# TensorE's order in the attention written out by hand, and other units without adaLN rows, in a hybrid decoder layer on one core

## The chip, the core and the metric

The kernel runs on one core of a Trainium2 chip. A core has several engines that run side by side, each with an instruction stream of its own that it works through in order: TensorE (PE in the profile; PEld is its loading of weights) multiplies matrices and writes into the small memory PSUM, VectorE (DVE) and ScalarE (ACT) do the elementwise work, GpSimd (POOL) does next to nothing here, and SyncE (SP) issues transfers. Streams wait for each other by semaphores. The metric is the device time of one execution in microseconds (us); lower is better.

## What is computed

One decoder layer on a sequence of 256 tokens with a model width of 2048, everything in float32. The reference, cut to what matters here:

```python
mod = jnp.dot(silu(c), w_ada[l]) + b_ada[l]                 # adaLN: 6 x 2048 values
shift1, scale1, gate1, shift2, scale2, gate2 = jnp.split(mod, 6, axis=-1)
h = _modulate(_rms_norm(x, norm1_g[l]), shift1, scale1)
proj = jnp.einsum("bsd,de->bse", h, w_in[l])
lru_x, lru_gate, q, k, v, g_a, g_b = jnp.split(proj, split_idx, axis=-1)
xc = _causal_depthwise_conv(lru_x, conv_w[l], conv_b[l])
rec = _rg_lru(xc, ...)                                      # two gate products, a scan over time
y_a = (rec * gelu(lru_gate)) @ w_lru_out[l]
att = _swa_sink_attention(q, k, v, attn_sinks[l], rel_bias) # 32 query heads, 4 kv heads, window 128
y_b = att @ w_attn_out[l]
merged = sigmoid(g_a) * y_a + sigmoid(g_b) * y_b
x = x + gate1 * (merged @ w_out[l])
h2 = _modulate(_rms_norm(x, norm2_g[l]), shift2, scale2)
x = x + gate2 * (square(relu(h2 @ w_ff1[l])) @ w_ff2[l])
return _rms_norm(x, final_g)
```

The attention adds a bias that depends on the distance, masks what lies outside the window, and its softmax has one more term, a sink value per head.

## The kernel before

**Products.** Activations lie with channels across the 128 partitions and the 256 tokens along the free dimension. For accuracy each float32 operand is split into a rounded part (`wh`, `hl[:, 0]`) and the rest (`wl`, `hl[:, 1]`), and a product is made of three matmuls. `gemm` (lines 196 to 207) does one tile of 128 output channels with three matmuls of 256 columns for each of its tiles of input channels; `gemm_wide` (line 220) does the same with one matmul of 512 columns and one of 256 (lines 229, 230, 232).

**Weights and units.** After a prologue the rest is a list of `units`. A unit takes 1 MB of weights. Its weights are loaded into one of 4 `raw` buffers (line 173, SyncE's queue), and then split in two halves of 1024 columns: ScalarE rounds (`w_round`, line 178, tile `wh`), VectorE takes the rest (`w_rest`, line 183, tile `wl`). `wh` and `wl` have 4 buffers each, so two units' worth. The main loop at the end of the function first loads and splits the weights of unit n + 2 and then runs unit n, so in the order of the program the split stands ahead of the unit's own work.

The prologue has already multiplied the first 8 of the 16 input tiles for the first 60 of 84 output tiles of the input projection. What is left of these goes two output tiles at a time: `gemm_pair` (line 240) calls `gemm` twice, with 24 matmuls each, and the first of the two uses the first half of the weights, the second the second half. The units are numbered so:

| units | what |
|---|---|
| 0, 1 | keys, values |
| 2 to 9 | queries: unit 2 + g gives the queries of group g (4 heads) |
| 10 to 17, 18 to 25 | the two halves of the recurrent branch (`lru_x`, `lru_gate`) |
| 26 to 29, 30 to 37 | first branch gate (pairs, then single wide tiles) |
| 38 to 53 | second branch gate |
| 54 to 69 (`n_ya` = 54) | first output projection, of the recurrent branch |
| 70 on | the attention's output projection, the joint one, the MLP |

**Attention.** For each of 8 groups of 4 heads, `att_scores` (line 651) loads the bias tile `bt` (one buffer, on ScalarE's queue), makes the scores on TensorE (16 instructions, line 669) into four PSUM banks, and the softmax: VectorE adds bias and finds the extreme (line 674), ScalarE takes the exponential (line 677), sums and the reciprocal follow (lines 680 to 683), and VectorE scales by it (line 687, eight instructions). `att_values` (line 691) turns the four heads' probabilities with 12 transposes on TensorE (line 702), which ScalarE copies out of PSUM (line 704), and multiplies them with the values (line 709, 16 instructions): for each pair of heads six transposes, two copies, eight products, one copy of the result (line 711).

**What sets the order.** The function only traces the instructions. A planner then makes each engine's stream: an instruction may be issued when its inputs and buffers are there by the planner's own estimate of times, and of those that may, the one traced earliest goes first. So an instruction can stand in the stream some way off its place in the program. `pin` (`tc.keep_in_program_order`) binds an instruction behind the one traced before it on its engine. In the input projection nothing on TensorE is pinned in the version before.

Elementwise work and the attention are put on a list `side` with a cost (`later`); after each unit the main loop traces from its front as long as there is `credit`, 2.3 per unit, at most 6. A query unit puts `att_values` of the group before (0.3) and `att_scores` of its own (2.5) on it; so in the program the scores of group g stand right after unit 2 + g. The recurrent branch (`lru_conv`, `lru_gates`, `lru_decay`, `lru_scan`, `lru_gelu`) is on the same list.

**Rows.** The 96 rows of the adaLN product are done one by one on VectorE: a row's weights (1 MB) come into one of the same four `raw` buffers (line 109), and one instruction multiplies and sums (`ada_unit`, line 283). The main loop adds a credit for rows with each unit (0.2 for the first 8 units, 0.6 for the next 10, then 0.1 and from unit 28 on 0.5) and issues as many as it covers: their loads ahead of the weights of unit n + 2, their sums after the unit. In quiet units it issues none and the credit stays. Before, the 8 units ahead of `n_ya` are quiet.

**Buffers.** The pool `kp` has 48 tiles (activations, results of the projections), `tp` 9 temporaries, `pa` four PSUM banks for the attention and other small products, `pg` four for the projections. At `n_ya` the recurrent branch's result is split into 16 tiles (`split`, lines 164 to 168) that take the places of the normed input `h`.

Of the kernel before, what the change touches and what calls it, by code (L numbers as in the profile page):

```python
# [12 lines left out]
AF = mybir.ActivationFunctionType  # L13
# [4 lines left out]
P = 128  # L18
# [9 lines left out]
W_IN_ORDER = (list(range(48, 50)) + list(range(50, 52)) + list(range(32, 48)) + list(range(0, 16))  # L28
              + list(range(16, 32)) + list(range(52, 68)) + list(range(68, 84)))
RAW_BUFS, WH_BUFS, WCH = 4, 4, 1024  # L30
LAG, CC, CG, CV, CS = 2, 1, .6, .3, 2.5
SSD = 4
EARLY, WARM = 6, 36

LAG, CC, CG, CV, CS = 2, 1.0, 0.6, 0.3, 2.5

ADA_LAST, QUIET_OUT, QUIET_FF1 = 0.3, 2, 3
LOOK, CREDIT, Z_FROM, QUIET_YA = 2, 2.3, 12, 8
ADA_RATES = 8 * [0.2] + 10 * [0.6] + 10 * [0.1] + 28 * [0.5]

ZN_FROM = 9
# [14 lines left out]
def _done(f):  # L56
    return max([k1 for k0, k1, n in PASSES if f < n], default=0)
# [9 lines left out]
def hybrid_layer(ctx: ExitStack, tc: tile.TileContext, x, xt, wada, w_p, w_r, w_f, vec, lruw, relb,  # L67
                 onehot, maskc, ident, out):
    nc = tc.nc
    te, ve, se = nc.tensor, nc.vector, nc.scalar  # L70
# [19 lines left out]
    def tmp(shape=(P, 2, T), dt=F32):  # L90
        return tp.tile(list(shape), dt, tag="t2", name=nm("t"))

    def bank(shape):
        return pa.tile(list(shape), F32, tag="pa", name=nm("pa"))


    pin = tc.keep_in_program_order
    vc = cp.tile([P, NV], F32, name="vc")
    idt = cp.tile([P, P], F32, name="idt")
# [5 lines left out]
    same = lambda i: i  # L105
# [87 lines left out]
    def w_load(src, n):  # L193
        return w_split(*w_dma(src, n))

    def gemm(parts, o, acts, ps=None):
        if ps is None:
            ps = pg.tile([P, T], F32, tag="pg", name=nm("pg"))
        n = len(acts)
        for k, hl in enumerate(acts):  # L200
            e = (o + k) * P
            wh, wl = parts[e // WCH]
            w = slice(e % WCH, e % WCH + P)
            te.matmul(ps, lhsT=wh[:, w], rhs=hl[:, 0], start=k == 0, stop=False)  # L204
            te.matmul(ps, lhsT=wh[:, w], rhs=hl[:, 1], start=False, stop=False)  # L205
            te.matmul(ps, lhsT=wl[:, w], rhs=hl[:, 0], start=False, stop=k == n - 1)  # L206
        return ps

    def gemm_late(parts, o, acts, pss, late):
# [27 lines left out]
        ve.tensor_tensor(out=t, in0=ps[:, 0], in1=t, op=ALU.add)  # L237
        return t

    def gemm_pair(parts, o, acts):  # L240

        ps = pg.tile([P, 2, T], F32, tag="pg", name=nm("pg"))
        for i in range(2):
            gemm(parts, o + i * len(acts), acts, ps[:, i])
        return ps

    full = [0]
# [46 lines left out]
    for q in range(4):  # L294
        pc = line_quarter(q)
        o = scr[:, q * 512:(q + 1) * 512]
# [39 lines left out]
    h = [None] * KT  # L336
# [114 lines left out]
    res, both = {}, {}  # L451
# [87 lines left out]
    for i in range(FRONT, len(p_units)):  # L539
        k0, k1, u, nf = p_units[i]  # L540
        split_w[i + 1] = split_unit(i + 1)
        w = split_w.pop(i)
# [5 lines left out]
        for j in range(nf if u or not k0 else 0):  # L548
            f = u + j
            if f % 2 == 0:  # L550
                open_ps[0] = pg.tile([P, 2, T], F32, tag="pg", name=nm("pg"))
            ps = open_ps[0][:, f % 2]
# [23 lines left out]
    units, side = [], []  # L576
# [8 lines left out]
    def later(cost, fn, *a):  # L585
        side.append((cost, fn, a))

    def in_unit(f, fin, nf=1):

        kd = _done(f)  # L590
        if kd:
            n = (KT - kd) * nf * P
            src = w_r[w_off[0]:w_off[0] + n * P].rearrange("(p n) -> p n", p=P)
            w_off[0] += n * P

            def run(w):
                if f == 0:
                    ps = pg.tile([P, 2, T], F32, tag="pg", name=nm("pg"))
                    gemm_late(w, 0, h[kd:], [(ps[:, 0], True, False), (ps[:, 1], False, True)], 2)
                    fin(f, ps, both[f])  # L600
                elif nf == 2:
                    fin(f, gemm_pair(w, 0, h[kd:]), both[f])
                else:
                    fin(f, gemm(w, 0, h[kd:]), res[f])
            add_unit(run, src, n)
        else:
            add_unit(lambda w: fin(f, gemm_wide(w, h), None))
# [9 lines left out]
    kd = [cp.tile([P, T], F32, name=f"kd{i}") for i in range(4)]  # L617
    vtok = cp.tile([P, 2, T], F32, name="vtok")
# [30 lines left out]
    ast = {}  # L649

    def att_scores(g):

        kv = g // 2
        bt = sp.tile([P, 4, T], F32, tag="bias", name=nm("bt"), bufs=1)
        se.dma_start(out=bt, in_=bass.AP(tensor=ud.tensor, offset=ud.offset + 4 * g * 384,
                                         ap=[[1, P], [384, 4], [1, T]]))
        st = sp.tile([P, 3, 8], F32, tag="ast", name=nm("as"), bufs=2)
        ng, dn, es = st[:, 0], st[:, 1], st[:, 2]
        ss = []
        sink = nsink[:, 8 * g:8 * g + 8]  # L660
        for t in range(2):
            q = res[F_Q + 2 * g + t]
            pss = [bank([P, 384]) for _ in range(2)]

            for qs, ks, sl in ((slice(0, 128), slice(128, 256), slice(0, 128)),
                               (slice(128, 256), slice(0, 256), slice(128, 384))):
                for i in range(2):
                    hd = slice(64 * i, 64 * i + 64)
                    te.matmul(pss[i][:, sl], lhsT=q[hd, qs], rhs=kd[kv][hd, ks], start=True, stop=True)
            for i in range(2):  # L670
                s = tmp([P, 384])
                for b, sl in HALVES:
                    c = 2 * (2 * t + i) + b
                    ve.tensor_tensor_reduce(out=s[:, sl], in0=pss[i][:, sl], in1=bt[:, 2 * t + i, 0:128 * (b + 1)],
                                            scale=1.0, scalar=sink[:, c:c + 1], op0=ALU.add, op1=ALU.min,
                                            accum_out=ng[:, c:c + 1])
                    table("exp", se.activation(s[:, sl], s[:, sl], AF.Exp, scale=-1.0, bias=ng[:, c:c + 1],
                                               accum_out=dn[:, c:c + 1]))
                ss.append(s)
        ve.tensor_tensor(out=es, in0=ng, in1=sink, op=ALU.subtract)  # L680
        table("exp", se.activation(es, es, AF.Exp))
        ve.tensor_tensor(out=dn, in0=dn, in1=es, op=ALU.add)
        ve.reciprocal(out=dn, in_=dn)
        for i in range(4):
            for b, sl in HALVES:
                c = 2 * i + b
                ve.tensor_scalar(out=ss[i][:, sl], in0=ss[i][:, sl], scalar1=dn[:, c:c + 1], scalar2=None, op0=ALU.mult)
        ast[g] = ss

    def att_values(g):  # L690

        kv = g // 2
        ss = ast.pop(g)
        vs = slice(64 * kv, 64 * kv + 64)
        for t in range(2):
            po = bank([P, T])
            pvs = []
            for i in (2 * t, 2 * t + 1):
                pt = bank([P, 384])

                for n, j in enumerate((0, 2, 1)):
                    te.transpose(pt[:, n * P:(n + 1) * P], ss[i][:, j * P:(j + 1) * P], idt)
                pv = tmp([P, 384])
                se.activation(pv, pt, AF.Copy)
                pvs.append(pv)

            for kb, cols, pc in ((1, slice(0, 256), slice(0, 256)), (0, slice(128, 256), slice(256, 384))):
                for i in range(2):
                    te.matmul(po[64 * i:64 * i + 64, cols], lhsT=vtok[:, kb, vs], rhs=pvs[i][:, pc],  # L709
                              start=kb == 1, stop=kb == 0)  # L710
            se.activation(res[F_Q + 2 * g + t], po, AF.Copy)

    def q_fin(f, ps, part):
        ve.scalar_tensor_tensor(out=part, in0=ps, scalar=-0.125, in1=part, op0=ALU.mult, op1=ALU.add)
        if f > 0:
            later(CV, att_values, f // 2 - 1)
        later(CS, att_scores, f // 2)
        if f == 14:
            later(CV, att_values, 7)


    lw, ri, ys, cv = {}, {}, {}, {}
# [401 lines left out]
    n_ya = len(units)  # L1124
    n_z = n_ya + 32 + Z_FROM
    n_ff1 = n_ya + 48
# [20 lines left out]
    for n, (run, src, size) in enumerate(units):  # L1147
        left = n_z - n
        if n < n_ya:
            ada_credit += size / 2048 * ADA_RATES[n]  # L1150
        else:
            ada_credit += max(0, 5 * KT - ada_next[0]) / left if left > 0 else ADA_LAST
        rows = 0
        if not (n_ya - QUIET_YA <= n < n_ya or n_ff1 - QUIET_OUT <= n < n_ff1 or n_ff1 + 16 - QUIET_FF1 <= n < n_ff1 + 16):
            while ada_credit > rows and ada_next[0] + rows < 6 * KT:
                rows += 1
            ada_credit -= rows
        for _ in range(rows):
            ada_dma()
        for j in range(n, min(n + LOOK + 1, len(units))):  # L1160
            if j not in ready:
                ready[j] = units[j][1]()
        if n == n_ya:
            flush()
        run(ready[n])
        ready[n] = None
        credit = min(credit + CREDIT * size / 2048, 6.0)
        while credit > 0 and side:
            cost, fn, a = side.pop(0)
            fn(*a)  # L1170
            credit -= cost
        while rows > 0 and ada_raw:
            ada_unit()
            rows -= 1
# [91 lines left out]
```

## Time and profile before

| | us |
|---|---|
| median of 3 runs | 1568.23 |
| lowest and highest run | 1567.98, 1568.62 |
| the profiled execution | 1566.39 |
| its span in the profile | 1564.6 |
| VectorE's busy share, ScalarE's | 82%, 59% |
| adaLN rows on VectorE (line 283) | 225.2 for 96, 2.35 each |
| splits of weights, ScalarE and VectorE (lines 178, 183) | 560.6 and 645.0 for 542 each |

How to read it: the profile comes from one execution, and the span is the time from its first to its last instruction; the device time lies a little above. A group of instructions is named by line, engine, operation, and the tiles that it writes and reads (out<-in), with its count. "Idle before" is the time in which the engine rested just before, and the name behind the arrow is what ended the rest. TensorE's matmuls overlap: one that is shown for 0.28 us may start every 0.12 us, so for TensorE the distance between starts tells more than busy time. A row of the windows view has the stretch, its length, then busy time and number of instructions for PE, PEld, DVE, ACT and POOL, TensorE's granted clock, the busy share of the DMA engines, and GB/s. A row of the timeline has start, length, engine, line, operation, tiles; instructions of one kind in a row are merged (x8). A row of the chain of waits has start, length and what it was.

### The profile page before, as it was taken

Reading aid. Unit: us, or ns where it says so; the run is one execution under the profiler, and the core shown is the slowest. Engines: PE = TensorE matmul, PEld = TensorE weight load, DVE = VectorE, ACT = ScalarE, POOL = GpSimd, SP = SyncE. Lnnn points to the kernel's source line nnn. Section 1 sums busy time; section 2 is a strip of 40 time slices with the busy share of each in tenths; the row PEclk is TensorE's granted clock in tenths of the full one; section 3 lists DMA queues with packets and bytes.
Section 4 is the critical chain, followed back from the end, with each engine's and each line's share of the span. In section 5 each row is a group of like instructions: output and inputs, shape, how many; then the busy total and the mean of one; then the engine's idle time right before and its main releaser. Section 6 shows DMA issues by size and latency. Waiting matters only on the chain.

```text
span 1564.6 us, 25672 instructions
## 1 busy us (share of the span) xinstructions
PE 1544.1 (99%) x10137; PEld 1397.7 (89%) x10137; DVE 1285.7 (82%) x2030; ACT 927.5 (59%) x1531; POOL 0.2 (0%) x4
## 2 busy tenths in 40 slices
PE   8999999999999999999999999999999999999998
PEld 7999998899988888888889988888888888888987
DVE  5898987898899689899898877888866888678785
ACT  5753457676786565444466763357644765357664
POOL 0000000000000000000000000000000000000000
PEclk9999999999999999999999999999999999999999
DMA  9998974566668669878987666866554566545551
GB/s 372 362 386 305 367 289 149 192 238 218 227 232 295 227 252 344 320 297 297 336 303 270 245 242 241 309 217 201 202 202 175 175 202 211 188 167 201 189 213 57
DMA packets 84744, 387.93 MB, mean 248 GB/s; under 512 B 7344, under 2 KB 36368, under 8 KB 44432
## 3 DMA queue, kind: packets, MB, share of 16 engines
q1 hardware_dynamic: 79632, 381.51, 66.8%
q10 hardware_dynamic: 4992, 4.79, 0.9%
q8 instruction: 79, 1.29, 0.3%
q14 instruction: 41, 0.34, 0.1%
HBM read 384.13 MB, written 2.15 MB: 247 GB/s over the span
## 4 chain that ended last, share of the span: by engine, by line
PE 90%; DVE 4%; DMA 2%; ACT 2%; issue 1%; ACTq 0%; SPq 0%; DVEq 0%
PE pg L230 40%; PE pg L229 19%; PE pg L206 6%; PE pg L204 5%; PE pg L205 5%; DMA ra<-in_wada_dram 2%; PE pg L232 1%; PE pa L937 1%; PE pa L939 1%; PE pa L938 1%; DVE ra L283 1%; PE pa L709 1%; PE pg L986 1%; PE pg L985 1%; PE pg L984 1%
## 5 line engine op out<-in xcount | busy, mean ns | idle before, releaser
L230 PE MATMUL pg<-k,wh 128*128 128x512 f32 x2832 | 981.4, 394 | 1.1 <-DVE k L167 1.1
L178 ACT ACTIVATE wh<-rw 128x1024 fp32r<-128x1024 f32 (+1 forms) x542 | 560.6, 1041 | 471.4 <-PE pg L230 320.3
L183 DVE TENSOR_TENSOR wl<-rw,wh 128x1024 fp32r<-128x1024 f32 (+1 forms) x542 | 645.0, 1201 | 169.6 <-ACT wh L178 162.9
L229 PE MATMUL pg<-k,wl 128*128 128x256 f32 x2655 | 743.2, 280 | 0.0
L230 PEld LDWEIGHTS pg<-k,wh 128*128 128x128 f32 x2832 | 521.6, 188 | 107.6 <-issue 1.4
L229 PEld LDWEIGHTS pg<-k,wl 128*128 128x128 f32 x2655 | 499.2, 188 | 8.5 <-ACT k L166 0.5
L204 PE MATMUL pg<-k,wh 128*128 128x256 f32 x878 | 248.6, 283 | 0.0
L205 PE MATMUL pg<-k,wh 128*128 128x256 f32 x878 | 246.6, 281 | 0.0
L206 PE MATMUL pg<-k,wl 128*128 128x256 f32 x878 | 246.2, 281 | 0.1
L283 DVE CUSTOM_DVE_ANT_0 ra<-ra,scr,vc 128x2048 f32<-128x2048 f32 x96 | 225.2, 2346 | 9.7 <-DMA ra<-in_wada_dram 8.0
L204 PEld LDWEIGHTS pg<-k,wh 128*128 128x128 f32 x878 | 165.3, 188 | 2.3 <-issue 2.1
L206 PEld LDWEIGHTS pg<-k,wl 128*128 128x128 f32 x878 | 165.1, 188 | 1.1 <-issue 0.7
L205 PEld LDWEIGHTS pg<-k,wh 128*128 128x128 f32 x878 | 165.1, 188 | 0.9 <-issue 0.7
L1103 DVE SCALAR_TENSOR_TENSOR k<-pg,mod,k 128x256 f32<-128x256 f32 x100 | 48.3, 483 | 18.6 <-PE pg L230 17.0
L237 DVE TENSOR_TENSOR t<-pg,t 128x256 f32<-128x256 f32 x127 | 53.0, 418 | 0.3 <-ACT t L236 0.3
L236 ACT ACTIVATE t<-pg 128x256 f32<-128x256 f32 x127 | 46.6, 367 | 7.6 <-PE pg L230 7.6
L232 PE MATMUL pg<-k,wl 128*128 128x256 f32 x177 | 49.8, 281 | 1.0 <-DVE wl L183 1.0
L232 PEld LDWEIGHTS pg<-k,wl 128*128 128x128 f32 x177 | 33.4, 189 | 9.0 <-DVE wl L183 1.8
L984 PE MATMUL pg<-z,wh 128*128 128x258 f32 x144 | 40.9, 284 | 0.0
L985 PE MATMUL pg<-z,wh 128*128 128x256 f32 x144 | 40.8, 284 | 0.0
L986 PE MATMUL pg<-z,wl 128*128 128x258 f32 x144 | 40.7, 283 | 0.0
L167 DVE TENSOR_TENSOR k<-t,k 128x256 fp32r<-128x256 f32 x80 | 33.7, 422 | 3.3 <-ACT k L166 3.3
(216 smaller groups left out, 1355.7 us busy)
## 6 DMA issues: line engine op xcount, KB each, us to landing
rw<-in_w_f_dram SPq DMA_DIRECT2D x188, 1024.0 KB, 4.9
ra<-in_wada_dram SPq DMA_DIRECT2D x96, 1024.0 KB, 5.9
rw<-in_w_r_dram SPq DMA_DIRECT2D x30, 1024.0 KB, 5.2
rw<-in_w_p_dram SPq DMA_DIRECT2D x29, 960.0 KB, 6.6
rw<-in_w_f_dram SPq DMA_DIRECT2D x48, 256.0 KB, 3.3
bt<-ud ACTq DMA_DIRECT2D x8, 512.0 KB, 3.7
k<-in_w_p_dram SPq DMA_DIRECT2D x9, 256.0 KB, 10.8
lw<-in_lruw_dram SPq DMA_DIRECT2D x4, 512.0 KB, 5.8
```

The costliest lines, as they stand in the source:

```text
L178: pin(se.activation(wh[:, :c], raw[:, o:o + c], AF.Copy))
L183: pin(ve.tensor_tensor(out=wl[:, :c], in0=raw[:, o:o + c], in1=wh[:, :c].bitcast(F32), op=ALU.subtract))
L204: te.matmul(ps, lhsT=wh[:, w], rhs=hl[:, 0], start=k == 0, stop=False)
L205: te.matmul(ps, lhsT=wh[:, w], rhs=hl[:, 1], start=False, stop=False)
L206: te.matmul(ps, lhsT=wl[:, w], rhs=hl[:, 0], start=False, stop=k == n - 1)
L229: te.matmul(ps[:, 0], lhsT=wl[:, w], rhs=hl[:, 0], start=False, stop=False)
L230: te.matmul(ps, lhsT=wh[:, w], rhs=hl, start=k == 0, stop=k == n - 1)
L232: te.matmul(ps[:, 0], lhsT=wl[:, w], rhs=hl[:, 0], start=False, stop=False)
L283: pin(ve.tensor_tensor_reduce(out=raw, in0=raw, in1=scr, scale=1.0, scalar=vc[:, V_BADA + c:V_BADA + c + 1], op0=ALU.mult, op1=ALU.add, ac ...
L984: te.matmul(ps, lhsT=wh[:, e], rhs=z[k][:, 0:258], start=k == 0, stop=False)
L985: te.matmul(ps[:, 0:256], lhsT=wh[:, e], rhs=z[k][:, 258:514], start=False, stop=False)
L986: te.matmul(ps, lhsT=wl[:, e], rhs=z[k][:, 0:258], start=False, stop=k == KT - 1)
```

## The change

The attention leaves the list `side`. From unit 3 on (`ATT = 3`), the units go in twos: in the middle of unit 3 + 2g, between the two tiles of its pair, the scores of group g are traced; in the middle of unit 4 + 2g the turns of group g, and after that unit its values. So the attention now runs from unit 3 to unit 18 instead of from unit 2 to about unit 10. All of TensorE's instructions of these units, of the scores, the turns and the values are pinned, so TensorE's stream there is the program's order. `att_values` is cut in two: `att_turns` makes the transposes of all four heads and their copies, one PSUM bank for each head, and `att_values` the products.

The list `side`, which now holds the recurrent branch only, is not worked on before unit 18 (`ATT + 15`); its credit is at its limit of 6 by then.

The quiet units around `n_ya` are now 4 before it and 3 from it on (50 to 56), where they were the 8 before it (46 to 53).

```diff
-LAG, CC, CG, CV, CS = 2, 1.0, 0.6, 0.3, 2.5
+LAG, CC, CG = 2, 1.0, 0.6
+ATT = 3
-LOOK, CREDIT, Z_FROM, QUIET_YA = 2, 2.3, 12, 8
+LOOK, CREDIT, Z_FROM, QUIET_YA = 2, 2.3, 12, 4
...
-    def gemm(parts, o, acts, ps=None):
+    def gemm(parts, o, acts, ps=None, pin=same):
...
-            te.matmul(ps, lhsT=wh[:, w], rhs=hl[:, 0], start=k == 0, stop=False)
+            pin(te.matmul(ps, lhsT=wh[:, w], rhs=hl[:, 0], start=k == 0, stop=False))
...
-    def gemm_pair(parts, o, acts):
+    def gemm_pair(parts, o, acts, between=None):
...
-            gemm(parts, o + i * len(acts), acts, ps[:, i])
+            gemm(parts, o + i * len(acts), acts, ps[:, i], pin if between else same)
+            if between and i == 0:
+                between()
...
     def in_unit(f, fin, nf=1):
 
         kd = _done(f)
+        g, step = divmod(len(units) - ATT, 2)
+        busy = 0 <= g < 8
+        between = None
+        if busy:
+            between = lambda: att_scores(g) if step == 0 else att_turns(g)
...
                 elif nf == 2:
-                    fin(f, gemm_pair(w, 0, h[kd:]), both[f])
+                    ps = gemm_pair(w, 0, h[kd:], between)
+                    if busy and step == 1:
+                        att_values(g)
+                    fin(f, ps, both[f])
...
-                    te.matmul(pss[i][:, sl], lhsT=q[hd, qs], rhs=kd[kv][hd, ks], start=True, stop=True)
+                    pin(te.matmul(pss[i][:, sl], lhsT=q[hd, qs], rhs=kd[kv][hd, ks], start=True, stop=True))
...
+    def att_turns(g):
+        ss = ast.pop(g)
+        pvs = []
+        for s in ss:
+            pt = bank([P, 384])
+            for n, j in enumerate((0, 2, 1)):
+                pin(te.transpose(pt[:, n * P:(n + 1) * P], s[:, j * P:(j + 1) * P], idt))
+            pv = tmp([P, 384])
+            se.activation(pv, pt, AF.Copy)
+            pvs.append(pv)
+        ast[g] = pvs
+
     def att_values(g):
-
         kv = g // 2
-        ss = ast.pop(g)
+        pvs = ast.pop(g)
         vs = slice(64 * kv, 64 * kv + 64)
         for t in range(2):
             po = bank([P, T])
...
                 for i in range(2):
-                    te.matmul(po[64 * i:64 * i + 64, cols], lhsT=vtok[:, kb, vs], rhs=pvs[i][:, pc],
-                              start=kb == 1, stop=kb == 0)
+                    pin(te.matmul(po[64 * i:64 * i + 64, cols], lhsT=vtok[:, kb, vs], rhs=pvs[2 * t + i][:, pc],
+                                  start=kb == 1, stop=kb == 0))
             se.activation(res[F_Q + 2 * g + t], po, AF.Copy)
 
     def q_fin(f, ps, part):
         ve.scalar_tensor_tensor(out=part, in0=ps, scalar=-0.125, in1=part, op0=ALU.mult, op1=ALU.add)
-        if f > 0:
-            later(CV, att_values, f // 2 - 1)
-        later(CS, att_scores, f // 2)
-        if f == 14:
-            later(CV, att_values, 7)
...
-        if not (n_ya - QUIET_YA <= n < n_ya or n_ff1 - QUIET_OUT <= n < n_ff1 or n_ff1 + 16 - QUIET_FF1 <= n < n_ff1 + 16):
+        if not (n_ya - QUIET_YA <= n < n_ya + 3 or n_ff1 - QUIET_OUT <= n < n_ff1 or n_ff1 + 16 - QUIET_FF1 <= n < n_ff1 + 16):
...
-        while credit > 0 and side:
+        while credit > 0 and side and n >= ATT + 15:
```

More of the change, by code (lines that the diff above doesn't have):

```diff
@@ L30 @@
 RAW_BUFS, WH_BUFS, WCH = 4, 4, 1024
-LAG, CC, CG, CV, CS = 2, 1, .6, .3, 2.5
 SSD = 4
 EARLY, WARM = 6, 36
-LAG, CC, CG, CV, CS = 2, 1.0, 0.6, 0.3, 2.5
+LAG, CC, CG = 2, 1.0, 0.6
+ATT = 3
 ADA_LAST, QUIET_OUT, QUIET_FF1 = 0.3, 2, 3
-LOOK, CREDIT, Z_FROM, QUIET_YA = 2, 2.3, 12, 8
+LOOK, CREDIT, Z_FROM, QUIET_YA = 2, 2.3, 12, 4
 ADA_RATES = 8 * [0.2] + 10 * [0.6] + 10 * [0.1] + 28 * [0.5]
@@ L203, in gemm @@
             w = slice(e % WCH, e % WCH + P)
-            te.matmul(ps, lhsT=wh[:, w], rhs=hl[:, 0], start=k == 0, stop=False)
-            te.matmul(ps, lhsT=wh[:, w], rhs=hl[:, 1], start=False, stop=False)
-            te.matmul(ps, lhsT=wl[:, w], rhs=hl[:, 0], start=False, stop=k == n - 1)
+            pin(te.matmul(ps, lhsT=wh[:, w], rhs=hl[:, 0], start=k == 0, stop=False))
+            pin(te.matmul(ps, lhsT=wh[:, w], rhs=hl[:, 1], start=False, stop=False))
+            pin(te.matmul(ps, lhsT=wl[:, w], rhs=hl[:, 0], start=False, stop=k == n - 1))
         return ps
@@ L696, in att_values @@
             po = bank([P, T])
[L697 to L705, printed above, removed]
             for kb, cols, pc in ((1, slice(0, 256), slice(0, 256)), (0, slice(128, 256), slice(256, 384))):
                 for i in range(2):
-                    te.matmul(po[64 * i:64 * i + 64, cols], lhsT=vtok[:, kb, vs], rhs=pvs[i][:, pc],
-                              start=kb == 1, stop=kb == 0)
+                    pin(te.matmul(po[64 * i:64 * i + 64, cols], lhsT=vtok[:, kb, vs], rhs=pvs[2 * t + i][:, pc],
+                                  start=kb == 1, stop=kb == 0))
             se.activation(res[F_Q + 2 * g + t], po, AF.Copy)
```

## The prediction

> **What bounds the kernel now.** I read the page's header first, then TensorE's waits, then windows, then the two stages that the diff touches, in order of time.
>
> ```profile
> span 1564.6 us, 25672 instructions
> PE 1544.1 (99%) x10137; PEld 1397.7 (89%) x10137; DVE 1285.7 (82%) x2030; ACT 927.5 (59%) x1531; POOL 0.2 (0%) x4
> PE pa L702 <- DVE t L687: 5.5, 7, 1.0
> PE pg L230 <- DVE k L167: 1.1, 1, 1.1
> PE pg L232 <- DVE wl L183: 1.0, 2, 0.7
> 217.90:319.60 101.70, 96.01 (x787) 81.96 (x786) 79.48 (x255) 68.74 (x203) 0.00 (x0) 1.00 0.54 191
> 560.00:600.00 40.00, 37.98 (x214) 32.30 (x213) 39.39 (x58) 23.38 (x48) 0.00 (x0) 1.00 0.83 316
> 320.00:560.00 240.00, 239.76 (x1637) 222.42 (x1636) 207.59 (x340) 173.36 (x290) 0.00 (x0) 1.00 0.65 233
> ```
>
> TensorE bounds the kernel: it is busy 99% of the span, and between 320 and 560 us it rests for 0.24 us. What can be won lies in two stretches. From 217.9 to 319.6 us, the attention, it rests 101.70 - 96.01 = 5.7 us, nearly all before the transposes of line 702. Around 570 us, the first output projection, two kinds of waits cost 2.1 us.
>
> Busy time hides more, so I count starts. [...] By busy time 5.7 us would be the most that the attention can give; by starts it is 12.8, as follows.
>
> ```profile
> 217.89 1.58 PE L669 MATMUL pa<-kd,k 64*128 64x128 f32 x16
> 219.40 0.39 PE L206 MATMUL pg<-k,wl 128*128 128x256 f32 x1
> 219.75 0.28 PE L205 MATMUL pg<-k,wh 128*128 128x256 f32 x1
> 227.62 0.28 PE L206 MATMUL pg<-k,wl 128*128 128x256 f32 x1
> 241.17 0.87 PE L709 MATMUL pa<-t,vtok 128*64 128x256 f32 x8
> 241.97 0.87 PE L702 MATMUL pa<-idt,t 128*128 128x128 f32 x6
> 242.60 0.36 PE L205 MATMUL pg<-k,wh 128*128 128x256 f32 x1
> L204 PE MATMUL pg<-k,wh 128*128 128x256 f32 x146 | 42.2, 289 | 0.0
> L206 PE MATMUL pg<-k,wl 128*128 128x256 f32 x145 | 41.7, 288 | 0.0
> L205 PE MATMUL pg<-k,wh 128*128 128x256 f32 x145 | 41.4, 286 | 0.0
> ```
>
> Between 219.75 and 227.62 stand 67 steps of the projection: 0.1175 us each. The attention's stretch holds 436 of these matmuls, some three of them only overlapping its edges: 433 x 0.1175 = 50.9 us. The other 50.8 us belong to eight groups of attention, 6.35 each. Uninterrupted, a group costs less: scores 219.40 - 217.89 = 1.5; six transposes 0.63, twelve 1.3; the values' eight instructions 0.80, twice 1.6; some 0.35 for the six changes of kind. That is 4.75 a group, 38.0 in all, and **12.8 us** lost now: waits at the turns, and transposes and values scattered in ones and twos between projection matmuls.
>
> **The change, part by part.** *The order of TensorE.* No arithmetic is added. All twelve transposes of a group come together in the middle of a unit, the scores in the middle of the unit before, the values after the unit. The changes of kind fall to a fixed few, which is inside the 4.75. So up to -12.8 us, if nothing waits.
>
> What can wait is the turn, and behind it, on TensorE, the other half of the unit, the values and everything later: the pinned order has nothing to put in between. From the first score to the turn there are 1.6 + 48 x 0.1175 = 7.24 us. Against that stands the softmax.
>
> ```profile
> 232.87 1.58 PE L669 MATMUL pa<-kd,k 64*128 64x128 f32 x16
> 233.83 0.35 DVE L674 CUSTOM_DVE_ANT_0 t<-pa,bt,nsink 128x128 f32<-128x128 f32 x1 [3.35 <-PE pa L669]
> 234.22 2.77 ACT t L677 x12
> 237.23 0.63 ACT t L677 x4
> 238.44 1.93 DVE L687 TENSOR_SCALAR t<-t,as 128x128 f32<-128x128 f32 x8
> 238.78 0.33 PE L702 MATMUL pa<-idt,t 128*128 128x128 f32 x1 [0.98 <-DVE t L687]
> 250.31 1.23 DVE L183 TENSOR_TENSOR wl<-rw,wh 128x1024 fp32r<-128x1024 f32 x1
> 251.45 0.68 DVE L714 SCALAR_TENSOR_TENSOR k<-pg,k 128x512 f32<-128x512 f32 x1
> L178 ACT ACTIVATE wh<-rw 128x1024 fp32r<-128x1024 f32 x19 | 19.8, 1052 | 3.8 <-PE pg L205 3.7
> ```
>
> Here nothing foreign stands in the chain: scores at 232.87, normalising from 238.44 (5.57 us later) for 1.93, the first transpose after 5.9 us. Against 7.24 that would be in time. But today the scores are traced after their unit, so the softmax outranks the next weights' split. In the new place they are traced after the split of unit n+2 and before the end of unit n. Each wh half is freed when unit n has used its half: the first exactly when the scores start, the second 24 matmuls (2.8 us) after they end. So the first half's wl (251.45 - 250.31 = 1.14 us) goes in among the reduces, and the second half's wh (1.05 us) among the exponentials. By those rows, in us from the first score: the exponentials end at 4.99 now (237.23 + 0.63 - 232.87), and normalising starts 0.58 after them. Of the 1.14 on VectorE, in the middle of its reduces, I let 0.85 reach them, and of the 1.05 on ScalarE all: they end at 6.9, the normalising runs from 7.5 to 9.4, and the last transposes end near 9.8 instead of 7.24 + 1.3 = 8.55. **1.2 us a group, 9.6 in all.** Bounds: 0.15 where the second half's split lands behind the normalising (it then ends at 8.3), 1.5 where it cuts it.
>
> *Conditioning rows in the softmax.* A row of the adaLN product holds VectorE for 2.35 us, and where it finds it free it goes in before the sum.
>
> ```profile
> 309.46 2.26 DVE ra L283
> 305.11 0.90 PE pa L669 x8
> 314.41 0.33 PE pa L702
> 247.95 2.35 DVE L283 CUSTOM_DVE_ANT_0 ra<-ra,scr,vc 128x2048 f32<-128x2048 f32 x1
> 290.16 2.35 DVE L283 CUSTOM_DVE_ANT_0 ra<-ra,scr,vc 128x2048 f32<-128x2048 f32 x1
> ```
>
> At 309.46 one lies in the chain, and the transposes come 9.3 us after the scores; at 247.95 too; at 290.16 the row fell outside. In units 3 to 18 seven rows are due. A row hurts when it lands between the scores and the last reduce, some 3.5 us of a period of 2 x 5.64 + 4.75 + 1.2 = 17 us: 7 x 3.5 / 17 = 1.4 rows, at 2.35 less the 0.6 that VectorE waits there anyway, 1.7 each: **+2.4**. Bounds: no row, and four rows (+6.8).
>
> *The turn's copies* take 0.5 each on ScalarE and have the 2.8 us half unit before the values: nothing. *The bias load* `bt` on ScalarE's queue, one buffer, now has a period of 17 us instead of 11.5:
>
> ```profile
> bt<-ud ACTq DMA_DIRECT2D x8, 512.0 KB, 3.7
> 500.00:520.00 20.00, 20.00 (x117) 17.53 (x116) 18.82 (x33) 13.28 (x26) 0.00 (x0) 1.00 0.84 315
> 520.00:540.00 20.00, 20.00 (x117) 17.59 (x116) 12.39 (x18) 10.82 (x19) 0.00 (x0) 1.00 0.49 169
> 540.00:560.00 20.00, 20.00 (x117) 17.54 (x116) 10.28 (x11) 9.48 (x14) 0.00 (x0) 1.00 0.57 201
> ```
>
> 3.7 us to land is covered. *The recurrent branch* starts at unit 18 instead of 10 and, by its credits (82 at 2.3 a unit, 6 saved up), ends at unit 51 instead of 45, so some 33 us later. What hides that is VectorE's rest between 520 and 560 us: 40 - 22.7 = 17 us, while TensorE stays full at VectorE's 18.8 of 20 before it. Nothing; without the cover the first output projection would wait for its inputs.
>
> *No rows around the first output projection.* Today the quiet units end just as it begins, and five saved rows come at once.
>
> ```profile
> 565.97 2.34 DVE L283 CUSTOM_DVE_ANT_0 ra<-ra,scr,vc 128x2048 f32<-128x2048 f32 x1
> 569.37 1.09 DVE L167 TENSOR_TENSOR k<-k,k 128x256 fp32r<-128x256 f32 x3
> 584.03 2.35 DVE L283 CUSTOM_DVE_ANT_0 ra<-ra,scr,vc 128x2048 f32<-128x2048 f32 x1
> 586.30 2.35 DVE L183 TENSOR_TENSOR wl<-rw,wh 128x1024 fp32r<-128x1024 f32 x2
> ```
>
> The row at 565.97 holds back the first split (569.37) on which TensorE waits 1.1 us, and that at 584.03 the weights at 586.30 (the 1.0 us). Afterwards the quiet units are 50 to 56, two rows move ahead to units 46 and 48, and the same credits give again five rows at unit 57. These also pass SP's queue, before the load of unit 59, with four raw buffers for rows and weights together; but no splits stand beside them there. A weight split (1.14) still precedes the first split: I leave 0.5 of the first wait and 0.2 for the new burst: **-1.4 us**. Bounds: -2.1, and 0 where the burst costs as much three units later.
>
> **Sum:** -12.8 + 9.6 + 2.4 - 1.4 = -2.2 us. The profiled execution took 1566.39 us, 1.8 more than its span and 1.8 less than the median of 1568.23. From the median: 1566.0. About 0.2% (3.1 us) is what a measurement of this kernel can tell from no change, so this is hardly to be told.
>
> **The rivals.**
>
> *The turns come in time.* If VectorE and ScalarE finish the softmax before the second half's split, the turn waits 0.15 x 8 = 1.2 us: -12.8 + 1.2 + 1.0 (rows, mostly taken up by the slack) - 1.4 = -12.0, **1556.2**. For it: 5.9 us against 7.24. Against it: all of today's waits have the same cause, TensorE's order planned for a shorter softmax than the chip ran (0.98 us at 238.78).
>
> *Slower: the rows sit in the softmax.* With four buffers a row is loaded when an earlier tile is freed; if that is the weight split at the end of a unit with values, it lands 5 us later, right after the next scores. Four such groups at 1.7 and turns at 1.5: -12.8 + 12.0 + 6.8 - 1.4 = +4.6, **1572.8**. With the turns at 1.5 it is slower than before from two such rows on, and by over 0.2% from about three. For it: 247.95 and 309.46. Against: 290.16.
>
> *The gate pairs run out of buffers.* At the last gates all 48 slots of `kp` are taken; the second gate's first pair needs a slot that the first two gelus free, now at unit 41 instead of 35, for an activation at unit 38. Four PSUM banks and nine temporaries carry that; if not, one unit of 5.6 us is lost: +3.4, **1571.6**.
>
> *The change does not do what it says:* the blocks stay as scattered as now, only the quiet units act: -1.4, **1566.8**.
>
> [...] No turn here rests that long, and the granted clock is 1.00 in every window above; I give it 1 in 100.
>
> **How the numbers follow.** The forecast's case, late turns (0.9 to 1.5 each) with none to three rows, has 0.55, and alone it reaches from 1561 to 1571: of it 0.19 is faster by over 0.2%, 0.31 the same, 0.05 slower. Turns in time: 0.22, faster. Rows in the softmax: 0.15, slower. Buffers: 0.04, half slower, half same. No effect of the order: 0.04, the same. Together faster 0.41, same 0.37, slower 0.22. The range takes in both large rivals' centres: 1556 to 1573; some 0.18 lie outside.
>
> **What would show it.** Right: blocks of 16, 12 and 16 on lines 669, 702 and 709; TensorE waiting at the turns for line 687 about 1.2 us, eight times, with an L183 among the reduces. In time: no such wait. Slower: L283 between L674 and L687 in three or more groups. The quiet units: no L283 from 565 to 576 us, and no wait for L167 over 0.5. It is wrong if the second half's split stands behind the normalising, or if L230 waits for a gate's activation before 560 us.

## The result, and the profile after

| | before | after |
|---|---|---|
| median, us | 1568.42 | 1584.73 |
| lowest and highest of 4 runs | 1567.98, 1570.67 | 1582.86, 1585.35 |
| span of the profiled execution | 1564.6 | 1583.6 |
| mean granted clock | 0.999 | 0.992 |

The ratio is 1.0099 [1.0082, 1.0117]: **16 us slower**, where 1566.0 was predicted and 1573 was the upper end of the range. The header of the page of after, and its waits of TensorE (engine, line, what it waited for, us in total, times, longest):

```profile
span 1583.6 us, 25657 instructions
...
PE 1549.5 (98%) x10137; PEld 1404.3 (89%) x10137; DVE 1288.6 (81%) x2030; ACT 935.3 (59%) x1536; POOL 0.2 (0%) x4
```

```profile
PE pa L706 <- DVE t L697: 16.5, 8, 3.4
...
PE pg L230 <- ACT wh L178: 2.1, 1, 2.1
PE pa L751 <- DVE t L743: 1.3, 1, 1.3
...
PE pg L232 <- DVE wl L183: 0.8, 1, 0.8
...
PE pg L230 <- DVE k L167: 0.3, 1, 0.3
```

In this kernel the scores are on line 679, the normalising is line 697, the turns 706, the values 720, the rows 285. The turns waited 5.5 us before and wait 16.5 now. But 11 us of new waits don't make 19.0 us of span (the spans are of single executions, of 1566.39 and 1585.35 us; the medians are 16.3 apart). Windows of after show a second thing, in the column of the granted clock (the third from the end):

```profile
252.00:256.00 4.00, 4.00 (x23) 3.88 (x22) 1.05 (x5) 1.97 (x4) 0.00 (x0) 0.57 0.68 266
294.00:298.00 4.00, 4.00 (x19) 3.92 (x20) 1.54 (x7) 1.96 (x4) 0.00 (x0) 0.50 0.80 330
314.00:318.00 4.00, 3.96 (x30) 3.47 (x31) 2.75 (x8) 1.90 (x4) 0.00 (x0) 1.00 0.74 262
```

Behind the long waits of the first four groups **TensorE runs at half its clock**: from 231.66 to 235.07, 252.15 to 255.56, 272.62 to 276.03 and 293.11 to 299.93 us windows of after show 0.50. Busy time doesn't tell it: 19 matmuls fill the 4 us from 294, where 30 stand in the 4 us from 314, behind a short wait. The timeline of after (start, length, engine, line; only the rows that decide) shows one group of each kind:

```profile
240.66 1.58 PE L679 MATMUL pa<-kd,k 64*128 64x128 f32 x16
...
241.90 1.22 DVE L183 TENSOR_TENSOR wl<-rw,wh 128x1024 fp32r<-128x1024 f32 x1
...
245.47 2.35 DVE L285 CUSTOM_DVE_ANT_0 ra<-ra,scr,vc 128x2048 f32<-128x2048 f32 x1
247.74 1.22 DVE L183 TENSOR_TENSOR wl<-rw,wh 128x1024 fp32r<-128x1024 f32 x1
248.95 0.68 DVE L725 SCALAR_TENSOR_TENSOR k<-pg,k 128x512 f32<-128x512 f32 x1
249.55 1.22 DVE L183 TENSOR_TENSOR wl<-rw,wh 128x1024 fp32r<-128x1024 f32 x1
...
251.12 1.93 DVE L697 TENSOR_SCALAR t<-t,as 128x128 f32<-128x128 f32 x8
251.46 2.69 PE L706 MATMUL pa<-idt,t 128*128 128x128 f32 x12 [3.36 <-DVE t L697]
...
305.50 1.58 PE L679 MATMUL pa<-kd,k 64*128 64x128 f32 x16
...
306.74 1.22 DVE L183 TENSOR_TENSOR wl<-rw,wh 128x1024 fp32r<-128x1024 f32 x1
...
311.04 1.04 ACT L178 ACTIVATE wh<-rw 128x1024 fp32r<-128x1024 f32 x1
312.12 1.23 DVE L183 TENSOR_TENSOR wl<-rw,wh 128x1024 fp32r<-128x1024 f32 x1 [0.93 <-ACT wh L178]
...
313.70 1.93 DVE L697 TENSOR_SCALAR t<-t,as 128x128 f32<-128x128 f32 x8
314.04 2.08 PE L706 MATMUL pa<-idt,t 128*128 128x128 f32 x12 [1.08 <-DVE t L697]
315.87 0.36 PE L204 MATMUL pg<-k,wh 128*128 128x256 f32 x1
...
323.38 0.38 PE L679 MATMUL pa<-kd,k 64*128 64x128 f32 x2
```

In the group at 240.66 an adaLN row (245.47) stands between the last reduce and the sums, with three weight splits around it; the normalising begins 10.5 us after the scores, and the turn waits 3.36 us. The group at 305.50 has no row: normalising after 8.2 us, a wait of 1.08 us. Even there the twelve transposes take 1.83 us (314.04 to 315.87) instead of the 1.3 that twelve were worked out at, since they follow the normalising (1.93 us) instruction by instruction: their row is 2.08 us long, and 1.48 in e5, where they don't wait (243.15). Groups 4 to 7 are of this second kind, groups 0 to 3 of the first.

### The profile page after: what moved, and what is told of

It is laid out like the page before. It is cut to its first block, busy times and chain, and to the rows that moved or that the text cites. A ratio compares the mean times of both kernels' runs of the same rounds, so it can differ in the third digit from the quotient of the medians.

```text
span 1583.6 us, 25657 instructions
## 1 busy us (share of the span) xinstructions
PE 1549.5 (98%) x10137; PEld 1404.3 (89%) x10137; DVE 1288.6 (81%) x2030; ACT 935.3 (59%) x1536; POOL 0.2 (0%) x4
## 4 chain that ended last, share of the span: by engine, by line
PE 91%; DVE 4%; DMA 2%; issue 1%; ACT 1%; SPq 0%; DVEq 0%; ACTq 0%
PE pg L230 40%; PE pg L229 19%; PE pg L204 6%; PE pg L206 6%; PE pg L205 6%; DVE wl L183 2%; DMA ra<-in_wada_dram 2%; PE pg L232 1%; PE pa L943 1%; PE pa L945 1%; PE pa L944 1%; PE pa L706 1%; PE pg L992 1%; PE pg L991 1%; PE pg L990 1%
## 5 line engine op out<-in xcount | busy, mean ns | idle before, releaser
L285 DVE CUSTOM_DVE_ANT_0 ra<-ra,scr,vc 128x2048 f32<-128x2048 f32 x96 | 225.3, 2347 | 17.0 <-DMA ra<-in_wada_dram 14.8
L684 DVE CUSTOM_DVE_ANT_0 t<-pa,bt,nsink 128x128 f32<-128x128 f32 x64 | 22.9, 413 | 20.2 <-PE pa L679 20.2
## 6 DMA issues: line engine op xcount, KB each, us to landing
k<-in_w_p_dram SPq DMA_DIRECT2D x9, 256.0 KB, 10.8
```

The lines of the kernel that those rows point to most:

```text
L285: pin(ve.tensor_tensor_reduce(out=raw, in0=raw, in1=scr, scale=1.0, scalar=vc[:, V_BADA + c:V_BADA + c + 1], op0=ALU.mult, op1=ALU.add, ac ...
```

## The experiments

What they had to tell apart: whether the time comes from the split of the weights, from the rows, from the quiet units, from the pins themselves, or from the clock. "us against before" is the difference of the medians of the same chip session.

| | median | us against before | ratio |
|---|---|---|---|
| e1 quiet units alone | 1569.74 | +2.8 | 1.0013 [1.0004, 1.0023] |
| e2 order alone | 1582.90 | +16.0 | 1.0111 [1.0095, 1.0128] |
| e3 rows behind the softmax | 1572.49 | +5.6 | 1.0040 [1.0025, 1.0056] |
| e4 split behind the scores | 1573.25 | +6.4 | 1.0037 [1.0024, 1.0050] |
| e5 = e3 and e4 | 1557.09 | -10.5 | 0.9935 [0.9920, 0.9950] |
| e6 no pins | 1567.72 | +0.1 | 1.0000 [0.9989, 1.0010] |
| e7 = e5, one row a unit | 1554.08 | -13.5 | 0.9916 [0.9901, 0.9931] |
| e8 turns half a unit later | 1557.03 | -10.6 | 0.9933 [0.9918, 0.9948] |
| e9 20 matmuls in the waits | 1582.71 | +15.2 | 1.0094 [1.0080, 1.0108] |
| e10 = e8, one row a unit | 1554.75 | -12.8 | 0.9915 [0.9902, 0.9929] |
| e11 10 matmuls in the waits | 1578.33 | +10.8 | 1.0067 [1.0053, 1.0081] |
| e12 = e10, branch not held back | 1570.95 | +3.4 | 1.0018 [1.0009, 1.0027] |

### e1, e2: the two parts of the change

e1 is the version before with only the quiet units moved; e2 is the version after with the old ones.

```diff
-LOOK, CREDIT, Z_FROM, QUIET_YA = 2, 2.3, 12, 8
+LOOK, CREDIT, Z_FROM, QUIET_YA = 2, 2.3, 12, 4
...
-        if not (n_ya - QUIET_YA <= n < n_ya or n_ff1 - QUIET_OUT <= n < n_ff1 or n_ff1 + 16 - QUIET_FF1 <= n < n_ff1 + 16):
+        if not (n_ya - QUIET_YA <= n < n_ya + 3 or n_ff1 - QUIET_OUT <= n < n_ff1 or n_ff1 + 16 - QUIET_FF1 <= n < n_ff1 + 16):
```

This is e1 against before; e2 against after is the same two lines the other way.

> The kernel before with only the quiet units moved (50 to 56 for 46 to 53). Theory 1 (rows and weight splits make the softmax late, TensorE waits at the pinned turns, and its clock falls after the long waits): the quiet units are a side matter; the five saved rows now hold back the weights of units 59 and 60, where the changed kernel waited 2.1 + 0.8 us, and the first wait of that stage goes from 1.1 to about 0.3 us: +1 to +2 us, 1570. Rival B (the new quiet units are what made it slower): +8 us or more, 1577.

> The changed kernel with the old quiet units (46 to 53). Theory 1: the attention's loss of some 15 us stays whole, the wait for line 697 at the turns stays at 16 us: 1582 to 1584. Rival B: 1572 or less.

The waits of e1:

```profile
PE pa L702 <- DVE t L687: 5.5, 7, 1.0
...
PE pg L230 <- ACT wh L178: 1.9, 1, 1.9
...
PE pg L232 <- DVE wl L183: 0.8, 1, 0.8
```

The wait for the first split (L167), 1.1 us before, has fallen to 0.3, but the saved rows now come at once at unit 57 and make TensorE wait 2.7 us there for a weight's halves: 3.0 in this stage, against 2.1 before. So the second part costs 0.6 to 3.6 us by its interval, where a gain of 1.4 was forecast. These waits needn't be all of it: e1's ten runs took 1566.87 to 1571.42 us, and the trace is of the shortest. The second part isn't the cause: e2 has all of the loss.

### e6: the pins

Everything of after, but nothing of the attention bound to the program's order.

```diff
-            gemm(parts, o + i * len(acts), acts, ps[:, i], pin if between else same)
+            gemm(parts, o + i * len(acts), acts, ps[:, i], same)
...
-                pin(te.transpose(pt[:, n * P:(n + 1) * P], s[:, j * P:(j + 1) * P], idt))
+                te.transpose(pt[:, n * P:(n + 1) * P], s[:, j * P:(j + 1) * P], idt)
```

(and the same at the scores and the values)

> The changed kernel with the same places in the program, but none of TensorE's instructions of the attention and its units pinned. Theory 1: the softmax is as late as in the changed kernel, since rows and splits still come into it, but the planner, which sees most of that, puts the next unit's matmuls into the gap; waits at the turns of about 1 us as before, 5 to 9 in all, no fall of the clock: 1566 to 1571. Rival C (the pins do not matter, the new places alone make the waits): 1580 or more.

```profile
PE pa L706 <- DVE t L697: 4.9, 8, 1.0
```

That is e6's wait at the turns. With the same places in the program but without pins the planner scatters the transposes again, the waits are those of before, and so is the time. What the change does lies in the pins.

### e3, e4, e5: what stands in the softmax

e3, the first diff, takes the rows of units 3 to 17 out of the softmax: they are issued behind the last normalising instruction traced. e4 traces the load and split of unit n + 2 behind unit n where that unit holds scores, so that the softmax outranks it. e5 does both.

```diff
-                ve.tensor_scalar(out=ss[i][:, sl], in0=ss[i][:, sl], scalar1=dn[:, c:c + 1], scalar2=None, op0=ALU.mult)
+                scaled[0] = ve.tensor_scalar(out=ss[i][:, sl], in0=ss[i][:, sl], scalar1=dn[:, c:c + 1], scalar2=None, op0=ALU.mult).ins
...
-            ada_unit()
+            if ATT <= n < ATT + 15:
+                with tc.issue_after(scaled[0]):
+                    ada_unit()
+            else:
+                ada_unit()
```

And e4:

```diff
-        for j in range(n, min(n + LOOK + 1, len(units))):
+        scores = ATT <= n < ATT + 16 and (n - ATT) % 2 == 0
+        for j in range(n, min(n + LOOK + 1 - scores, len(units))):
...
         run(ready[n])
+        if scores:
+            ready[n + LOOK] = units[n + LOOK][1]()
```

> The changed kernel, with each adaLN row of units 3 to 17 bound on VectorE behind the scaling of the group that was traced last. Theory 1: no row stands between the reduces and the scaling any more, the first four turns wait 1.2 us like the last four (16.5 us in all become 8 to 9), the granted clock stays at 1.00 through the attention, and the attention is 12 to 14 us shorter: 1571, within 2. Rival A (turns and scores stand too close for this softmax whatever VectorE does between): the first four turns still wait over 2 us, 1580 or more.

> The changed kernel, with the load and split of unit n + 2's weights traced behind unit n where that unit holds scores, so that the softmax goes before the split on VectorE and ScalarE. Theory 1: the last four turns wait less than 0.3 us instead of 1.2, the first four, which keep their row, 1.2 less than the 2.4 to 3.4 us of the changed kernel, and so no rest is long enough for the clock to fall: 1570 to 1574. Rival A: all eight turns wait as in the changed kernel, 1583 or more.

> Both edits on the changed kernel: rows bound behind the scaling, and the split of unit n + 2's weights traced behind a unit with scores. Theory 1: all eight turns in time (wait for line 697 under 0.5 us in all), the turns' twelve transposes in 1.2 us, clock 1.00; the attention costs 4.75 us a group as forecast, 14 to 16 us less than with the rows alone: 1557 within 2. Rival A: 1.2 us stay at each turn, 1570.

e3's wait at the turns and its attention (start, length, busy times, clock):

```profile
PE pa L707 <- DVE t L698: 8.6, 8, 1.1
```

```profile
219.90:359.70 139.80, 131.18 (x1102) 117.39 (x1101) 104.16 (x279) 84.95 (x216) 0.00 (x0) 1.00 0.56 199
```

Without rows all eight waits are alike, 1.1 us, and the clock stays at 1.00 through the attention. The same 1102 matmuls took 153.70 us in after (next fence): the rows, with the clock that falls behind them, cost 13.9 us.

```profile
220.20:373.90 153.70, 137.21 (x1102) 124.51 (x1101) 103.61 (x279) 85.28 (x216) 0.00 (x0) 0.94 0.54 185
```

e4's waits, and windows of 4 us behind its first four turns:

```profile
PE pa L706 <- DVE t L697: 7.7, 4, 1.9
```

```profile
231.00:235.00 4.00, 4.00 (x23) 4.00 (x22) 0.85 (x1) 0.77 (x2) 0.00 (x0) 0.58 0.74 289
249.00:253.00 4.00, 3.65 (x27) 3.17 (x28) 3.06 (x10) 1.90 (x4) 0.00 (x0) 1.00 0.97 381
268.00:272.00 4.00, 3.97 (x20) 3.77 (x21) 2.75 (x8) 1.96 (x4) 0.00 (x0) 0.57 1.01 412
288.00:292.00 4.00, 4.00 (x21) 3.63 (x22) 2.62 (x8) 1.96 (x4) 0.00 (x0) 0.62 1.00 403
```

With the split out of the way the four groups without a row don't wait at all, which shows the split as their cause; the four with a row wait 1.9 each. That the clock still fell behind three of these four was not expected, since the waits are little over half of after's longest. The waits don't stand alone, though: the transposes come right behind them, and in all four groups no projection matmul runs for 3.8 to 4.3 us; in e3, where the clock stays up, for 2.9.

e5 has no wait at the turns left. Two starts of scores in its timeline:

```profile
235.87 0.38 PE L680 MATMUL pa<-kd,k 64*128 64x128 f32 x2
251.85 0.38 PE L680 MATMUL pa<-kd,k 64*128 64x128 f32 x2
```

These are the first two of each group's sixteen. A group and its 96 projection matmuls take 15.98 us (96 x 0.1175 = 11.28, so the group 4.70). It takes 17.88 in after without a row (305.50 to 323.38).

### e9, e11: the price of the clock

To part the clock from the waits, matmuls of constants, whose result is not used, are put on TensorE ahead of the turns of groups 0 to 3: 20 in e9 (below), 10 in e11. The softmax comes as late as in after, but TensorE doesn't rest so long.

```diff
     def att_turns(g):
         ss = ast.pop(g)
+        if g < 4:
+            fill = pg.tile([P, 2, P], F32, tag="pg", name=nm("pg"))
+            for _ in range(20):
+                pin(te.matmul(fill[:, 0], lhsT=ones, rhs=ones, start=True, stop=True))
```

> The changed kernel with 20 matmuls of 128 columns on a constant (0.11 us each, 2.2 us, their result is not used) ahead of the turns of the first four groups, where TensorE rests for 2.4 to 3.5 us; rows and splits as in the changed kernel. If the rest makes the clock fall: the softmax is as late, the rest at these turns shrinks to 0.2 and 1.3 us, the granted clock stays at 1.00 in the attention, and 4 us behind the turns and 2 in the transposes are saved: 1578 to 1580. If the clock falls for another reason (the transposes themselves, the load on TensorE): no gain, 1584.

> The kernel with matmuls in the wait, with 10 instead of 20: each ran as two instructions of 0.11 us, so 20 took 4.46 us, longer than any wait, and 10 take 2.2. If the rest makes the clock fall: the rests at the first four turns are 0.2 to 1.4 us, the granted clock stays at 1.00 in the attention, and against the changed kernel the slow matmuls behind the turns are saved, 5 to 7 us: 1578 to 1580. If rests of 1.4 us already make it fall: 1582 or more, with a clock under 1.00 behind these turns.

e9 missed: each of these matmuls runs as two instructions (160 in the trace for 80 in the program), 20 take 4.46 us, longer than the waits, and what the clock gives they cost. e11 fits into them. Its timeline at group 2 and its windows behind the first four turns:

```profile
266.80 2.39 PE L705 MATMUL pg<-ones 128*128 128x128 f32 x20
270.32 2.08 PE L710 MATMUL pa<-idt,t 128*128 128x128 f32 x12 [1.13 <-DVE t L697]
```

```profile
232.00:236.00 4.00, 4.00 (x38) 3.65 (x38) 1.52 (x2) 1.72 (x4) 0.00 (x0) 1.00 0.60 254
250.00:254.00 4.00, 3.78 (x28) 3.29 (x29) 1.80 (x8) 1.90 (x4) 0.00 (x0) 1.00 0.84 338
270.00:274.00 4.00, 3.68 (x27) 3.19 (x28) 1.90 (x8) 1.90 (x4) 0.00 (x0) 1.00 0.86 336
290.00:294.00 4.00, 3.58 (x26) 3.09 (x27) 1.97 (x9) 1.90 (x4) 0.00 (x0) 1.00 0.88 360
```

The turn at 270.32 still comes 3.5 us after the half unit's end at 266.80, but TensorE rests only the last 1.13 of it, and the clock stays at 1.00. e11 beats after by 6.4 us of the medians, by 5.5 where each is set against the version before of its own session; in the two traces groups 0 to 3 take 79.30 us (220.45 to 299.75) against 85.34 (220.16 to 305.50). So **the price of the fallen clock** is some 6 us.

### e7, e8, e10, e12: what makes the pinned order pay

e7 is e5 with at most one row a unit, against the burst of e1. e8 leaves the rows and splits as in after, but moves the turns from the middle to the end of unit 4 + 2g, and the values to the end of unit 5 + 2g. e10 is e8 with one row a unit. e12 is e10 without the condition that holds the recurrent branch back to unit 18.

```diff
-            while ada_credit > rows and ada_next[0] + rows < 6 * KT:
+            while ada_credit > rows and rows < 1 and ada_next[0] + rows < 6 * KT:
```

That is the cap of e7 and e10. The places of e8 and e10:

```diff
-        busy = 0 <= g < 8
+        busy = 0 <= g < 9
...
-        if busy:
-            between = lambda: att_scores(g) if step == 0 else att_turns(g)
+        if busy and g < 8:
+            between = lambda: att_scores(g) if step == 0 else None
...
-                    if busy and step == 1:
-                        att_values(g)
+                    if busy and step == 1 and g < 8:
+                        att_turns(g)
+                    if busy and step == 0 and g > 0:
+                        att_values(g - 1)
```

And e12, against e10:

```diff
-        while credit > 0 and side and n >= ATT + 15:
+        while credit > 0 and side:
```

> The kernel with both edits, and at most one adaLN row in a unit, so that the rows saved in the quiet units are spread over the units behind them. Theory 1: the two waits at units 59 and 60 (about 3 us in all, for the weights' rounding and rest) go, 2.5 to 3.5 us below the kernel with both edits: 1554. Rival D (these waits come from the splits of the attention's result that run there, not from the rows): no change against the kernel with both edits.

> The changed kernel with the turns at the end of the unit where they stood in its middle, and the values at the end of the next; rows and splits as in the changed kernel. Theory 1: the turn has 2.8 us more, so the last four turns do not wait and the first four wait 1 us or less, no fall of the clock; 1565 within 3. Rival A: the same time as theory 1; what tells them apart is that with a row the wait is 2.3 us longer than without.

> The changed kernel with the turns half a unit later and at most one adaLN row in a unit. Theory 1: the gains add, as they did for the kernel with both edits: 3 us below the kernel with the later turns alone, 1554. If the rows that are still in the softmax or the later values cost something elsewhere: above 1556.

> The kernel with the later turns and one row a unit, with the recurrent branch's work on the list taken up as soon as there is any (from unit 10), not from unit 18. Theory 1: its short operations (0.4 to 0.6 us) also get between the reduces and the scaling of groups 4 to 7, but the later turns have 2.8 us for that, so no wait for the scaling over 0.5 us; the one wait of 1.1 us for the convolution near 428 us goes or stays small: 1553 to 1556, the same. If holding the branch back is what made the later turns free of waits: waits of 1 us at the turns of groups 4 to 7, 1558 or more.

e8's timeline at its second group:

```profile
239.45 2.35 DVE L285 CUSTOM_DVE_ANT_0 ra<-ra,scr,vc 128x2048 f32<-128x2048 f32 x1
...
243.97 1.93 DVE L699 TENSOR_SCALAR t<-t,as 128x128 f32<-128x128 f32 x8
...
246.41 0.38 PE L708 MATMUL pa<-idt,t 128*128 128x128 f32 x2
```

The row is still in the softmax, but the turn at 246.41 finds the normalising done (243.97 + 1.93) and doesn't wait. Waits of up to 1 us there and a time of 1565, 8 us longer, had been expected; the 2.8 us of slack of 24 more matmuls (24 x 0.1175) cover everything: none of e8's waits is at the turns. The cap of one row a unit brings 3.0 us from e5 to e7 and 2.3 from e8 to e10: e7's waits of lines 230 and 232 have shrunk to 0.3 us, where e5 has 2.9 and, behind them, a granted clock of 0.50 from 588.16 to 591.57 us; e7's is 1.00 in that stage. **e7 and e10 beat both kernels**, by about 0.85% the one before.

e12 was expected to stay near e10, and is 16 us slower. Its waits:

```profile
PE pa L753 <- ACT t L743: 5.5, 1, 5.5
...
PE pa L753 <- DVE t L745: 2.9, 2, 1.8
PE pa L722 <- DVE as L686: 2.6, 2, 1.6
PE pa L753 <- ACT t L757: 1.3, 2, 0.9
PE pa L754 <- DVE as L686: 1.1, 1, 1.1
```

Lines 753 and 754 are the gate products of the recurrent branch. They aren't pinned themselves, but they are traced between pinned units, and the matmuls traced next are bound behind them. So TensorE stands 13.4 us in these rows: 8.4 until a convolution is ready (lines 743, 745), 5.0 until a sigmoid of the branch or a reduce of the softmax is through (lines 757, 686). In the longest wait the clock falls too, for 10.24 us:

```profile
293.13:303.37 10.24, 4.92 (x11) 3.54 (x12) 10.14 (x32) 6.25 (x14) 0.00 (x0) 0.50 0.42 154
```

That the pins are the way is read from the program and these waits; no run took them from this place. Holding the branch back, which looked like housekeeping, is a needed part of a pinned order. None of these waits is at the turns (line 708).

## Why the prediction was wrong

**Right.** The blocks are 16, 12 and 16, and the order itself is worth what was said: 4.70 us a group in e5 against the 4.75 of the working, 50.8 - 8 x 4.70 = 13.2 us against 12.8. A split among the reduces and one later make the turn late (e4). No transfer and no buffer stood in the way; the first split's wait fell to 0.3 (0.5 forecast).

**Wrong, first: the term "late turns", 1.2 each and 9.6 in all.** A group without a row costs 17.88 - 15.98 = 1.9 us, 15.2 in all. The working let the normalising start 7.5 us after the scores; it starts at 8.2. It counted the second half's rounding on ScalarE among the exponentials (311.04, as it came), but not that half's split on VectorE, which then stood (312.12, 1.23) directly ahead of the second sum. The upper bound of 1.5 was too low for the same reason. The slow transposes were in the working, which reckons to the end of the last one: 9.8 us after the first score, where it is 10.4 (315.87 - 305.50).

**Wrong, second: the term "rows in the softmax", 1.4 rows by a uniform landing, +2.4.** The first four groups have one each. They took from 220.2 to 305.50, 21.3 us each, that is 5.3 more than in e5: 1.9 for lateness, 3.4 for the row. A row's load gets its buffer when a weight's is freed, and so it lands in step with the units, not anywhere in the period; the rival that turned slower had named just this, and got 0.15. That it lands in step is read from four rows at the same place, 4.8 us after the scores, not tried by itself. The trace of before already spoke against the uniform landing. The working took three of its rows, two in the chain and one outside; the attention holds two more, and both lie between the last reduce and the second sum:

```profile
221.88 2.35 DVE L283 CUSTOM_DVE_ANT_0 ra<-ra,scr,vc 128x2048 f32<-128x2048 f32 x1
273.47 2.35 DVE L283 CUSTOM_DVE_ANT_0 ra<-ra,scr,vc 128x2048 f32<-128x2048 f32 x1
```

That is four of five, with the normalising at 227.42 and 277.19, 9.5 and 8.1 us after these groups' scores. In after the rows cost 13.9 us by e3, of which some 6.4 are the clock (e11); what is left, 7.5, is 1.9 a row, near the 1.7 of the working. So the count was wrong, not the price.

Scores of the first group, from the view of line 679 in after (duration, then first and last start):

```profile
L679 PE MATMUL pa<-kd,k x128: 269/374/378, 220.2 to 360.3; 64*128 64x128 f32 x64, 64*128 64x256 f32 x64
```

**Wrong, third: the clock, 1 in 100, "no turn here rests that long".** The chance was for a fall of TensorE's clock behind a rest at a turn. That no rest would be long enough followed from the two sizes above: with the lateness and a row, rests of 2.2 to 3.4 us came out. Half clock (0.50) for 3.41 us behind three of them and 6.82 behind the fourth cost some 6 us together. No run shows how long a rest has to be for that: e4 has falls behind rests of about 1.9 us, but with the transposes behind them there is no projection matmul for 3.8 us or more, and no run has such a rest without the transposes. The length of the rest alone doesn't decide: the one of e4's four that escaped lasts as long as the others (247.41 to 249.34), and in e2 the first turn rests for 2.2 us and the clock stays at 1.00, where after's falls behind a rest as long. It isn't shown either why the falls of after's first four groups begin six times 3.41 us apart (231.66, 252.15, 272.62, 293.11), and those of e4 (230.95, 268.50, 288.98) eleven and six times. What decides stays open.

**Wrong, fourth: the quiet units, -1.4.** Of the two ends given, even 0 was too low by e1's interval: the burst at unit 57 costs 2.7 us of waits (e1). The sum had left 0.2 for it since "no splits stand beside them there"; the weights' own splits do.

With the measured sizes the sum is -13.2 + 15.2 + 7.5 + 6.4 = +15.9 for the attention. Measured: after's window of 153.70 us holds 1102 matmuls, less the attention's 352 that is 750 of the projection, 88.1 us; 65.6 are left for the attention, against 50.8: +14.8. The other 4.2 of the 19.0 us of span are not all told apart: a new wait of line 751 (1.3; a row at 453.99 us holds a convolution up) and the first output projection, whose waits are 3.2 now against 2.1 and behind whose burst the clock is not full either (0.50 from 617.37 to 620.78):

```profile
600.00:620.00 20.00, 17.10 (x91) 14.52 (x90) 19.91 (x28) 7.79 (x11) 0.00 (x0) 0.93 0.98 387
```

As for the rivals: the slower one was the right direction and mechanism; its 1572.8 lacks the clock (6.4) and 3.2 us of lateness (it had 12.0, measured 15.2), 9.6 of the 11.9 us up to 1584.7, and it has the forecast's -1.4 for the quiet units, which cost time. "Turns in time" is what e5 and e8 are, 1557, and needs another edit. "No effect of the order" is e6.

## What to carry to other kernels

A pinned order takes away the planner's filler: whatever comes late then stops the engine, and everything that stands between two pinned instructions is bound too. So reckon the slack of a pinned consumer with all that may stand ahead of it on the other engines' streams, the last split included, and with regular transfers landing at the worst place each time; then put the consumer one half unit later, or bind the foreign work behind the chain. And don't save work up around a place that is to be quiet: here one row a unit brought 2.3 and 3.0 us, and moving the quiet units brought a loss.

## What was not expected of the hardware

TensorE's granted clock fell to a half behind three of four rests of about 1.9 us, each with the transposes right behind it (e4), and behind none of 1.1 with the same transposes (e3, e11). It fell for 3.41 us or a multiple, 6.82 once in after and 10.24 in e12. So after's four long waits, 12 us of rest, came some 6 us dearer, and hardly any of that is seen as idle time: in the two slow windows shown TensorE is 100% busy, and only the clock's column tells it. And each of the ten matmuls of 128 x 128 x 128 on a float32 constant that e11 has at a turn runs as two instructions: they are the 20 in the row at 266.80, 0.11 us each.
